# Memory attention of a two-block transformer: queries by features, the query norm in the exponential, two token halves

## The chip, the cores and the metric

The kernel runs on one core of one Trainium2 chip. The metric is the device time of one execution in microseconds (us). The kernel before took 2875.79 us, the median of 3 runs (2870.99 to 2877.94).

## The reference

The input is 512 tokens of 1024 features in fp32. A first block (gated delta rule and dilated window attention) is followed by two layers that each hold a feed-forward network (FFN), a mixer of three attentions, a memory attention, a second FFN and a norm. The change is in the memory attention, which runs once in each of the two layers:

```
h = rms_norm(x, mem_norm_x);  m = rms_norm(mem, mem_norm_m)        # 512 tokens; 256 memory rows
q = rms_norm(per head of (h @ w_q), q_gain)                        # 4 heads of 64
k = rms_norm(per head of k, k_gain);  k, v = split(m @ w_kv)
p = softmax(q k^T * 64**-0.5)                                      # 512 x 256 for each head
x = x + (p v) @ w_o                                                # 256 -> 1024
```

Each rms_norm divides by the square root of the mean square plus 1e-6.

## The kernel before

The residual x lies in the core's memory by features: eight tiles of 128 features by 512 tokens (`X(0)` to `X(7)`). A large product is made of three matmuls for each group of 128 inputs, since weights and activations are each split into a high part, which the matmul takes, and a low rest (`split`, `chunk3`: ScalarE writes the high part, lines 366, 376 and 379, VectorE the rest, lines 367, 377 and 380). `gemm_f` (lines 388 to 390) gives its result by features, `gemm_t` (lines 411 to 413) by tokens. Partial sums have eight banks in three pools: `acc` (3), `ss` (2) and `st` (3).

`Norm` (norm_split) splits x as soon as each `X(k)` is final and adds up its squares on GpSimd (lines 488 and 493); the factor of each token, `norm.cols()`, comes from matmuls with a column of ones (line 434), one small VectorE instruction (424) and a power on GpSimd (425).

`memory` (line 1711), before the change:

- Queries: four products of 128 tokens (three in `acc`, one in `ss`; 96 matmuls of 256 columns). For each of them `query` copies the result out times the token's factor (1726), `head_norm` squares it (1337), reduces by head (1338), takes the power (424, 425) and multiplies (1340), and `place` turns it to features (two transposes, 418) and splits it into `qT` with the gains as scale (379, 380).
- Items: class `Attn` with `per=2` makes eight items, one for each of four token tiles and each of two head pairs (h and h + 2). An item has three stages. Scores: six matmuls of 256 columns, one head after the other, into one `ss` bank (1157 to 1159), one row maximum for both heads (1169), two exponentials with row sums (1172). Turn: four transposes (418) and a VectorE copy (1207). Values: eight records of 64 columns (1224); after both items of a token tile one reciprocal (1234) and one multiplication (1237).
- Output: `turned` transposes and splits each token tile (418, 376, 377); `out(0)` and `out(1)` multiply each half of the tokens with `w_o` (48 matmuls each of 256 columns, 388 to 390, into `acc`) and add into x (1759). `out(0)` is a background generator, stepped between items.

What comes ahead is the mixer's last output product (`out_proj("mla")`, matmuls of 512 columns into `ss`, added into x on line 1658); what comes after is the second FFN, whose first products (lines 400 to 402) need x after `out(1)`. Its weights, and those of w_q and w_o, pass through the same four buffers for high parts, four for low parts and two for raw data.

The order written in the code is not the order on the engines. The framework plans each engine's order ahead with a model of durations: an instruction that is written later goes first where the earlier ones are not ready in that model. On the chip each engine then runs its list in that order.

Of the kernel before, what the change touches and what calls it, by code (L numbers as in the profile page):

```python
# [11 lines left out]
AF = mybir.ActivationFunctionType  # L12
OP = mybir.AluOpType
AX = mybir.AxisListType

T = 512
D = 1024
KD = D // 128
# [4 lines left out]
EPS = 1e-6  # L23
# [7 lines left out]
def _cols(v, n):  # L31
    return np.ascontiguousarray(v.reshape(n, 128).T)
# [96 lines left out]
def prep(I):  # L129
    I = {k: np.asarray(v) for k, v in I.items()}  # L130
    A = {}
# [4 lines left out]
    p = Packer()  # L136
    p.add("ident", np.eye(128))
    p.add("ones", np.ones((128, 128)))
    p.add("norm_w", _cols(I["norm_w"][0], KD))
    for l in range(L2):  # L140
        for n in ("ffn1_norm", "mix_norm", "mem_norm_x", "mem_norm_m", "ffn2_norm", "block_norm", "grp_out_gain"):
# [3 lines left out]
        for n, d in (("mla", 64), ("swa", 64), ("na", 64), ("mem", 64)):  # L145
            for s in "qk":
                g = I[f"{n}_{s}_gain_2"][l]
                if n == "mla":
                    c = np.ones(128, np.float32)
                    c[:64] = g[:64]  # L150
                    p.add(f"{n}{s}r{l}", _rows(g[64:96]))
                else:
                    c = np.concatenate([g, g])
# [5 lines left out]
    t = I["conv_w"][0][:, 0, :]  # L159
    p = Packer()  # L160
# [4 lines left out]
    a = np.arange(128)  # L165
# [7 lines left out]
    p = Packer()  # L173
# [11 lines left out]
    p = Packer()  # L185
    p.add("swab", _bias_swa())
    c, s = _rope_tables(10000.0)
# [5 lines left out]
    w = I["w_in"][0]  # L193
# [5 lines left out]
    o = 2056  # L199
# [42 lines left out]
class Prog:  # L242
# [268 lines left out]
def nat(i):  # L511
    return lambda t: t[:, i * 128:(i + 1) * 128]
# [11 lines left out]
def bc(col, n):  # L524

    return col[:, :, None].to_broadcast([128, col.shape[1], n])
# [6 lines left out]
def hs(h):  # L533
    return slice(h * 128, (h + 1) * 128)
# [796 lines left out]
def head_norm(g, z, nh, d):  # L1331

    nc = g.nc
    sq = g.b()[:, :nh * d]
    zv, sv = z.rearrange("p (h d) -> p h d", h=nh), sq.rearrange("p (h d) -> p h d", h=nh)
    m = g.small(2 * nh)
    nc.scalar.activation(sq, z, AF.Square)
    nc.vector.reduce_sum(m[:, :nh], sv, axis=AX.X)
    g.rsqrt(m[:, nh:2 * nh], m[:, :nh], 1.0 / d)
    nc.vector.tensor_tensor(zv, zv, bc(m[:, nh:2 * nh], d), op=OP.mult)  # L1340


def gain_col(g, name, l, scale):
    t = g.small(1)
    g.nc.vector.scalar_tensor_tensor(t, g.c(f"{name}qg{l}"), scale, g.c(f"{name}kg{l}"), op0=OP.mult, op1=OP.mult)
    return t
# [362 lines left out]


def memory(g, l, xt, mem):
    nc, A = g.nc, g.A
    X = tview(xt)
    norm = g.norm_split(X, g.c(f"mem_norm_x{l}"))
    wh, wl = g.chunk3(A[f"memq{l}"][0], 8)
    qT = g.h(F32R)
    gq = gain_col(g, "mem", l, 0.125)

    def place(i, z):
        ps = g.st()  # L1720
        g.turn(ps, lambda hp: z[:, hs(hp)], 2)
        g.split(ps[:, :256].rearrange("p (k t) -> p k t", k=2), qT[:, :2, hs(i)], qT[:, 2:, hs(i)], gq)

    def query(i, ps):
        z = g.b()[:, :256]
        nc.scalar.activation(z, ps[:, :256], AF.Copy, scale=norm.cols()[:, i:i + 1])
        head_norm(g, z, 4, 64)
        g.later(2, place, i, z)


    pss = [g.acc() for i in range(3)]
    for ks in (range(6), range(6, KD)):
        for i in range(3):
            g.gemm_t(pss[i][:, :256], norm.parts, nat(i), wh, wl, 0, 256, ks)
            if ks[-1] == KD - 1:
                query(i, pss[i])
                g.tick()
    half = lambda t, hb: t[hb * 64:hb * 64 + 64]
    o = g.h()
    hi, lo = g.h(F32R), g.h(F32R)  # L1740
    w = {}

    def turned(i):
        ps = g.st()
        g.turn(ps, lambda c: o[:, i, hs(c)], 2)
        kv = ps[:, :256].rearrange("p (k t) -> p k t", k=2)
        g.split(kv, hi[:, 0:2, hs(i)], lo[:, 0:2, hs(i)])
        if i == 1:
            g.bg.append(out(0))

    def out(hf):
        if not w:
            w["o"] = g.chunk3(A[f"memo{l}"], 2)
        c = slice(hf * 256, hf * 256 + 256)
        parts = [(hi[:, k, c], lo[:, k, c]) for k in range(2)]
        for k in range(KD):
            ps = g.acc()[:, :256]
            g.gemm_f(ps, *w["o"], k * 128, k * 128 + 128, parts)
            nc.vector.tensor_tensor(X(k)[:, c], X(k)[:, c], ps, op=OP.add)
            yield  # L1760

    at = Attn(g, 4, 64, lambda h, i: tuple(half(qT[:, c + h // 2, hs(i)], h % 2) for c in (0, 2)),
              lambda h: [half(t[:, (h // 2) * 256:(h // 2) * 256 + 256], h % 2) for t in mem.kT],
              lambda t, h: mem.v[:, t * 256 + h * 64:t * 256 + h * 64 + 64], lambda i: o[:, i, :256],
              lambda i: (0, 2), None, None, lambda i: g.later(1, turned, i), per=2)
    ps = g.ss()
    g.gemm_t(ps[:, :256], norm.parts, nat(3), wh, wl, 0, 256)
    query(3, ps)
    g.tick()
    g.pipe(at.items(), steps=2)  # L1770
    g.flush()
    for _ in out(1):
        pass
# [98 lines left out]
```

## Time and profile before

| | |
|---|---|
| median of 3 runs | 2875.79 us |
| profiled execution, its own time | 2872.66 us |
| its span, first to last instruction | 2870.9 us |
| mean granted TensorE clock | 0.988 |
| TensorE (PE) busy | 2803.3 us (98%) |
| VectorE (DVE) busy | 1453.1 us (51%) |
| ScalarE (ACT) busy | 1161.7 us (40%) |
| GpSimd (POOL) busy | 459.5 us (16%) |

Some 1.8 us of the profiled execution's time lie outside its span. Busy time of PE is modelled from pipelined matmuls, so that a stretch can read as wholly busy at either level of the clock; a clock of 1.00 is 2.4 GHz, 0.50 is 1.2 GHz. The memory attention lies at 1367 to 1423 us in the first layer and at 2444 to 2493 us in the second.

### The profile page before, as it was taken

To read this page: it belongs to the slowest core of one execution; us is meant where nothing else is said; L and a number is where in the kernel's file an instruction comes from. 1 tells how busy PE (TensorE), PEld (TensorE's weight loads), DVE (VectorE), ACT (ScalarE), POOL (GpSimd) and SP (SyncE) were. 2 spreads that over 40 slices of the span, in tenths; PEclk is the share of its full clock that TensorE was granted. 3 is DMA by queue.
4 is the path that set the end of the run, shared out by engine and by line. 5 is a ranking of instruction groups with operands and counts; after the bars stand their busy time and mean duration, and the time that the engine had idled before them with its cause. 6 is when DMAs were issued, how large, how long until landed. Compare 5 with 4: busy or idle time off the path is not lost.

```text
span 2870.9 us, 37996 instructions
## 1 busy us (share of the span) xinstructions
PE 2803.3 (98%) x15101; PEld 2379.5 (83%) x15101; DVE 1453.1 (51%) x2339; ACT 1161.7 (40%) x2007; POOL 459.5 (16%) x556
## 2 busy tenths in 40 slices
PE   8999999999999999999999999999999999999998
PEld 6798999888888888777888888888888767888887
DVE  5734445445433444677653444533444677653442
ACT  4323444533322234765432224322334766432232
POOL 4422222002000013412200002000013412200001
PEclk9999999999999999999899999999999999999998
DMA  4111222233323232211132323223232211123322
GB/s 162 45 45 60 80 68 74 74 100 126 96 88 103 94 106 68 70 40 64 38 109 86 106 86 105 92 88 107 94 106 67 71 41 65 56 97 88 103 89 80
DMA packets 78466, 239.63 MB, mean 83 GB/s; under 512 B 8528, under 2 KB 14800, under 8 KB 78160
## 3 DMA queue, kind: packets, MB, share of 16 engines
q1 hardware_dynamic: 78288, 237.20, 25.9%
q8 instruction: 119, 1.95, 0.3%
q14 instruction: 59, 0.48, 0.1%
HBM read 235.06 MB, written 2.10 MB: 83 GB/s over the span
## 4 chain that ended last, share of the span: by engine, by line
PE 91%; DVE 4%; ACT 2%; issue 1%; POOL 1%; DMA 0%; SPq 0%; DVEq 0%; ACTq 0%; POOLq 0%
PE ss L388 12%; PE ss L390 12%; PE ss L389 12%; PE acc L388 8%; PE acc L390 8%; PE acc L389 8%; PE acc L411 4%; PE acc L413 4%; PE acc L412 4%; PE st L418 2%; PE acc L1224 2%; PE ss L1260 2%; PE acc L401 1%; PE acc L402 1%; PE acc L400 1%
## 5 line engine op out<-in xcount | busy, mean ns | idle before, releaser
L367 DVE TENSOR_TENSOR wl<-raw,wh 128x1024 fp32r<-128x1024 f32 (+4 forms) x448 | 508.8, 1136 | 563.3 <-ACT wh L366 562.5
L366 ACT ACTIVATE wh<-raw 128x1024 fp32r<-128x1024 f32 (+3 forms) x459 | 450.1, 981 | 725.4 <-PE ss L389 537.2
L388 PE MATMUL acc<-x,wh 128*128 128x512 f32 x1040 | 407.7, 393 | 9.3 <-ACT wh L366 8.8
L390 PE MATMUL acc<-x,wl 128*128 128x512 f32 x1040 | 408.8, 393 | 0.1
L389 PE MATMUL acc<-x,wh 128*128 128x512 f32 x1040 | 407.4, 392 | 0.0
L388 PE MATMUL ss<-h,wh 128*128 128x512 f32 (+1 forms) x843 | 328.9, 391 | 0.3 <-DVE h L1658 0.3
L389 PE MATMUL ss<-h,wh 128*128 128x512 f32 (+1 forms) x843 | 326.3, 389 | 0.2 <-DVE h L380 0.2
L390 PE MATMUL ss<-h,wl 128*128 128x512 f32 (+1 forms) x843 | 325.9, 388 | 0.0
L493 POOL TENSOR_TENSOR b<-b 128x512 f32<-128x512 f32 (+1 forms) x77 | 107.3, 1394 | 1160.7 <-ACT b L488 1069.3
L388 PE MATMUL ss<-x,wh 128*128 128x512 f32 x680 | 264.6, 389 | 0.1
L390 PE MATMUL ss<-x,wl 128*128 128x512 f32 x680 | 264.7, 389 | 0.0
L389 PE MATMUL ss<-x,wh 128*128 128x512 f32 x680 | 264.5, 389 | 0.0
L411 PE MATMUL acc<-wh,x 128*128 128x256 f32 (+1 forms) x880 | 252.8, 288 | 0.0
L412 PE MATMUL acc<-wl,x 128*128 128x256 f32 (+1 forms) x880 | 252.6, 288 | 0.0
L388 PEld LDWEIGHTS acc<-x,wh 128*128 128x128 f32 x1040 | 196.1, 189 | 50.9 <-ACT wh L366 8.8
L413 PE MATMUL acc<-wh,x 128*128 128x256 f32 (+1 forms) x816 | 232.0, 286 | 0.0
L390 PEld LDWEIGHTS acc<-x,wl 128*128 128x128 f32 x1040 | 196.0, 188 | 41.7 <-DVE wl L367 0.9
L389 PEld LDWEIGHTS acc<-x,wh 128*128 128x128 f32 x1040 | 196.0, 189 | 40.3 <-issue 0.3
L388 PEld LDWEIGHTS ss<-h,wh 128*128 128x128 f32 x843 | 159.6, 190 | 33.8 <-DVE h L1658 0.8
L389 PEld LDWEIGHTS ss<-h,wh 128*128 128x128 f32 x843 | 159.8, 190 | 32.7 <-DVE h L380 1.0
L390 PEld LDWEIGHTS ss<-h,wl 128*128 128x128 f32 x843 | 159.7, 189 | 32.0
L1101 ACT ACTIVATE b<-b 128x512 f32<-128x512 f32 x88 | 55.6, 632 | 310.5 <-DVE b L1100 310.4
(384 smaller groups left out, 4756.9 us busy)
## 6 DMA issues: line engine op xcount, KB each, us to landing
raw<-in_ffn_a SPq DMA_DIRECT2D x176, 512.0 KB, 3.6
raw<-in_ffn_b SPq DMA_DIRECT2D x64, 384.0 KB, 3.1
raw<-in_ffn_b SPq DMA_DIRECT2D x64, 320.0 KB, 2.9
raw<-in_w_swa SPq DMA_DIRECT2D x36, 512.0 KB, 3.9
raw<-in_w_gate SPq DMA_DIRECT2D x16, 512.0 KB, 3.6
raw<-in_w_qkv SPq DMA_DIRECT2D x12, 512.0 KB, 4.2
raw<-in_mixN SPq DMA_DIRECT2D x12, 512.0 KB, 3.6
raw<-in_mixA SPq DMA_DIRECT2D x8, 544.0 KB, 3.6
```

Source lines behind the costliest of these rows:

```text
L366: nc.scalar.activation(h[:, s], r[:, s], AF.Copy)
L367: low.tensor_tensor(l[:, s], r[:, s], h[:, s].bitcast(F32), op=OP.subtract)
L388: mm(ps, a, xh, start=first and k == 0, stop=False)
L389: mm(ps, a, xl, start=False, stop=False)
L390: mm(ps, b, xh, start=False, stop=last and k == n - 1)
L411: mm(ps, a, wh[k][:, c0:c1], start=k == 0, stop=False, **part)
L412: mm(ps, a, wl[k][:, c0:c1], start=False, stop=False, **part)
L413: mm(ps, b, wh[k][:, c0:c1], start=False, stop=k == n - 1, **part)
L418: self.nc.tensor.transpose(ps[:, i * 128:(i + 1) * 128], src(i), self.ident)
L493: (engine or nc.gpsimd).tensor_tensor(acc, acc, sq, op=OP.add)
L1224: nc.tensor.matmul(self.pso[:, c:c + d], PT[:, hs(j * n + k)], self.v(lo + k, hj), start=k == 0, stop=k == n - 1)
L1260: nc.tensor.matmul(v3(s), self.q[h // 4][:96, i, hs(h % 4)], self.k[h // 4][:96, :, hs(h % 4)], start=True, stop=True)
```

## The change

Only `memory` changes, and one constant is added: `pair`, 128 rows by 2 columns, which marks the two 64-row heads of a feature tile.

- Queries are made by features with `gemm_f`, in four parts: c (two head pairs: heads 2c and 2c + 1 are the two 64-row halves of the tile) by hf (two halves of 256 tokens). Both c of one hf share one `acc` bank. The result goes unnormalised, times the gains, into `qT`. There is no copy by tokens, no `head_norm` and no transposition of queries.
- The norm's factor: the squares of the raw queries (ScalarE) are summed by head with `pair` as the moving operand (two matmuls of two columns for each part); with e, made from the column sums of the squares of x, one VectorE instruction and one power give f for 2 token tiles by 2 heads. f multiplies the negated row maximum and is the scale of the exponential. `norm.cols()` is not called.
- An item is now a token tile and a feature tile c. Its two heads write two `ss` banks, their matmuls in turn; each has its own row maximum. Reciprocal and multiplication come with every item.
- The order is written out: the items of the first token half stand between pieces of the products of the second half (`nx()`, six matmuls each), those of the second half between pieces of `out(0)`.

```diff
+    def products(c, hf, k0, k1):
+        if (c, k0) == (0, 0):
+            bank[hf] = g.acc()
+        g.gemm_f(bank[hf][:, hh[c]], wh[k0:k1], wl[k0:k1], c * 128, c * 128 + 128, xs[hf][k0:k1], k0 == 0, k1 == KD)
+        if k1 == KD:
+            g.split(bank[hf][:, hh[c]], qT[:, c, hh[hf]], qT[:, 2 + c, hh[hf]], gq)
+            st["sq", c, hf] = sq = g.b()[:, :256]
+            nc.scalar.activation(sq, bank[hf][:, hh[c]], AF.Square)
+
+    def factors(c, hf):
+        if (c, hf) == (0, 0):
+            nc.vector.tensor_scalar(e, g.col_sums(norm.acc, [nat(i) for i in range(4)]), EPS / D, EPS * EPS, op0=OP.mult, op1=OP.add)
+        ps, sq, fc = g.st(), st.pop(("sq", c, hf)), fv(c, hf)
+        for i in range(2):
+            nc.tensor.matmul(ps[:, 2 * i:2 * i + 2], sq[:, hs(i)], pair, start=True, stop=True)
+        two = lambda t: t.rearrange("p (i j) -> p i j", i=2)
+        nc.vector.scalar_tensor_tensor(two(fc), two(ps[:, :4]), 1.0 / 64, bc(e[:, 2 * hf:2 * hf + 2], 2), op0=OP.mult, op1=OP.add)
+        nc.gpsimd.tensor_tensor(fc, fc, g.half.to_broadcast([128, 4]), op=OP.pow)
+
+    def scores(c, i):
+        st["m", c, i] = m = g.small(8)
+        P = st["p", c, i] = g.p()
+        ss = [g.ss()[:, :256] for j in range(2)]
+        for a, b in ((0, 0), (0, 1), (1, 0)):
+            for j, s in enumerate(ss):
+                nc.tensor.matmul(s, half(qT[:, 2 * a + c, hs(i)], j), half(mem.kT[b][:, c * 256:c * 256 + 256], j),
+                                 start=a + b == 0, stop=a == 1)
+        for j, s in enumerate(ss):
+            nc.vector.tensor_reduce(m[:, j:j + 1], s, axis=AX.X, op=OP.max, negate=True)
+        fi = fv(c, i // 2)[:, i % 2 * 2:i % 2 * 2 + 2]
+        nc.vector.tensor_tensor(m[:, 0:2], m[:, 0:2], fi, op=OP.mult)
+        for j, s in enumerate(ss):
+            nc.scalar.activation(P[:, j * 256:j * 256 + 256], s, AF.Exp, bias=m[:, j:j + 1], scale=fi[:, j:j + 1],
+                                 accum_out=m[:, 2 + j:3 + j])
...
+    products(0, 0, 0, KD)
+    products(1, 0, 0, 4)
+    factors(0, 0)
+    scores(0, 0)
+    products(1, 0, 4, KD)
+    w["o"] = g.chunk3(A[f"memo{l}"], 2)
+    unit = iter([(lambda c=c, k=k: products(c, 1, k, k + 2)) for c in range(2) for k in range(0, KD, 2)])
+    nx = lambda: next(unit)()
+    scores(0, 1)
+    nx()
+    turn(0, 0)
+    nx()
+    factors(1, 0)
+    scores(1, 0)
+    turn(0, 1)
+    nx()
+    values(0, 0)
+    scores(1, 1)
+    nx()
...
+    turned(0)
+    scores(0, 3)
+    nx()
+    turned(1)
+    o0 = out(0)
+    turn(0, 2)
+    next(o0)
+    factors(1, 1)
+    scores(1, 2)
+    turn(0, 3)
+    next(o0)
...
+    values(1, 3)
+    turned(2)
+    next(o0)
+    turned(3)
+    next(o0)
     g.flush()
     for _ in out(1):
         pass
```

`turn` (four transposes, VectorE copy) and `values` (matmuls of 64 columns into an `acc` bank) keep their instructions.

## Rows read from the trace of the kernel before

**Rows 1.** The page's busy line.
```profile
PE 2803.3 (98%) x15101; PEld 2379.5 (83%) x15101; DVE 1453.1 (51%) x2339; ACT 1161.7 (40%) x2007; POOL 459.5 (16%) x556
```
**Rows 2.** Busy time by stretch, first layer; then PEclk, DMA share, GB/s.
```profile
1367.29:1376.05 8.76, 8.72 (x73) 8.51 (x71) 3.08 (x5) 3.59 (x5) 2.94 (x3) 1.00 0.18 60
1376.05:1380.79 4.74, 0.00 (x1) 0.04 (x1) 4.30 (x11) 3.69 (x9) 1.62 (x2) 0.97 0.49 156
1380.79:1401.00 20.21, 19.73 (x90) 16.37 (x90) 10.67 (x22) 7.87 (x29) 2.32 (x3) 0.50 0.04 16
1401.00:1422.69 21.69, 21.01 (x171) 20.06 (x171) 14.83 (x30) 8.15 (x20) 2.48 (x2) 1.00 0.01 1
```
**Rows 3.** Busy time by stretch, second layer.
```profile
2443.69:2452.13 8.44, 8.44 (x72) 8.39 (x70) 3.78 (x5) 3.27 (x5) 2.94 (x3) 1.00 0.20 64
2452.13:2457.18 5.05, 0.15 (x2) 0.03 (x1) 3.60 (x11) 4.01 (x9) 1.61 (x2) 0.85 0.54 168
2457.18:2462.60 5.42, 4.94 (x24) 3.38 (x24) 3.36 (x8) 2.38 (x8) 2.33 (x3) 0.51 0.09 37
2462.60:2492.61 30.01, 29.54 (x238) 27.53 (x237) 21.66 (x45) 13.75 (x42) 2.48 (x2) 1.00 0.00 1
```
**Rows 4.** Matmuls in order of time: an early query product; both stages' ends.
```profile
1352.49 0.40 PE L411 MATMUL acc<-wh,x 128*128 128x256 f32 x2
...
1367.29 0.28 PE L411 MATMUL acc<-wh,x 128*128 128x256 f32 x1
...
1422.57 0.28 PE L390 MATMUL acc<-h,wl 128*128 128x256 f32 x1
...
2443.69 0.28 PE L411 MATMUL acc<-wh,x 128*128 128x256 f32 x1
```
**Rows 5.** TensorE's waits: us in total, times, longest.
```profile
PE st L418 <- DVE s L424: 9.7, 2, 4.9
```
**Rows 6.** The chain that ended last, first layer, while TensorE stands.
```profile
1376.05 1.06 ACT wh L366
...
1377.13 1.23 DVE wl L367
1378.36 0.66 DVE s L1338 x2
...
1379.17 2.00 POOL s L425 x2
```
**Rows 7.** Groups of the second layer's stage: count, busy us, mean ns.
```profile
L1207 DVE COPY pt<-st 128x512 f32<-128x512 f32 x8 | 5.4, 681 | 0.7 <-PE st L418 0.6
L1169 DVE TENSOR_REDUCE s<-ss 128x2 f32<-128x512 f32 x8 | 5.3, 684 | 0.9 <-PE ss L1159 0.7
L380 DVE SCALAR_TENSOR_TENSOR h<-st,s,h 128x256 fp32r<-128x256 f32 x4 | 1.9, 480 | 1.4 <-ACT h L379 1.4
L1234 DVE RECIPROCAL s<-s 128x4 f32<-128x4 f32 x4 | 0.7, 166 | 0.0
...
L1172 ACT ACTIVATE p<-ss,s 128x256 f32<-128x256 f32 x16 | 7.5, 474 | 4.3 <-DVE s L1169 4.3
...
L379 ACT ACTIVATE h<-st,s 128x256 fp32r<-128x256 f32 x4 | 1.9, 478 | 2.1 <-PE st L418 2.1
L1337 ACT ACTIVATE b<-b 128x256 f32<-128x256 f32 x4 | 1.7, 414 | 0.1
...
L425 POOL TENSOR_TENSOR s<-s,half 128x4 f32<-128x4 f32 x4 | 3.9, 1010 | 3.5 <-DVE s L424 3.5
```
**Rows 8.** Matmuls in order of time: paired scores (mixer), transposes, values.
```profile
1137.43 0.62 PE L1188 MATMUL ss<-h 64*128 64x256 f32 x6
...
2474.04 1.04 PE L418 MATMUL st<-cst,p 128*128 128x128 f32 x8
...
2475.15 1.89 PE L1224 MATMUL acc<-b,pt 128*128 128x64 f32 x16
```
**Rows 9.** Busy time by stretch in the mixer: a wait, and the clock behind it.
```profile
1190.70:1192.25 1.55, 0.00 (x0) 0.00 (x0) 1.55 (x5) 1.55 (x8) 1.55 (x2) 1.00 0.00 0
1192.25:1196.10 3.85, 3.84 (x16) 3.84 (x17) 3.40 (x15) 3.07 (x12) 2.47 (x3) 0.57 0.73 237
```

More of the change, by code (lines that the diff above doesn't have):

```diff
@@ L138, in prep @@
     p.add("ones", np.ones((128, 128)))
+    p.add("pair", np.arange(128)[:, None] // 64 == np.arange(2))
     p.add("norm_w", _cols(I["norm_w"][0], KD))
@@ L1717, in memory @@
     gq = gain_col(g, "mem", l, 0.125)
[L1719 to L1737, printed above, removed]
+    pair = g.c("pair")
+    f = g.small(16)
+    fv = lambda c, hf: f[:, 8 * hf + 4 * c:8 * hf + 4 * c + 4]
+    e = g.small(4)
+    st = {}
+    hh = [slice(0, 256), slice(256, 512)]
+    xs = [[(a[:, c], b[:, c]) for a, b in norm.parts] for c in hh]
+    bank = {}
+    def products(c, hf, k0, k1):
[15 more added lines that the diff above has]
+        nc.gpsimd.tensor_tensor(fc, fc, g.half.to_broadcast([128, 4]), op=OP.pow)
     half = lambda t, hb: t[hb * 64:hb * 64 + 64]
@@ L1741, in memory, with turn, values @@
     w = {}
+    def scores(c, i):
[13 more added lines that the diff above has]
+                                 accum_out=m[:, 2 + j:3 + j])
+    def turn(c, i):
+        P, t = st.pop(("p", c, i)), g.st()
+        g.turn(t, lambda k: P[:, hs(k)])
+        st["t", c, i] = PT = g.pt()
+        nc.vector.tensor_copy(PT, t)
+    def values(c, i):
+        PT, m = st.pop(("t", c, i)), st.pop(("m", c, i))
+        ps = g.acc()[:, :128]
+        for j in range(2):
+            v = (2 * c + j) * 64
+            for k in range(2):
+                nc.tensor.matmul(ps[:, j * 64:j * 64 + 64], PT[:, hs(2 * j + k)], mem.v[:, k * 256 + v:k * 256 + v + 64],
+                                 start=k == 0, stop=k == 1)
+        nc.vector.reciprocal(m[:, 4:6], m[:, 2:4])
+        dst = o[:, i, hs(c)]
+        hv = lambda t: t.rearrange("p (j d) -> p j d", j=2)
+        nc.vector.tensor_tensor(hv(dst), hv(ps), bc(m[:, 4:6], 64), op=OP.mult)
     def turned(i):
@@ L1747, in turned @@
         g.split(kv, hi[:, 0:2, hs(i)], lo[:, 0:2, hs(i)])
-        if i == 1:
-            g.bg.append(out(0))
     def out(hf):
-        if not w:
-            w["o"] = g.chunk3(A[f"memo{l}"], 2)
-        c = slice(hf * 256, hf * 256 + 256)
+        c = hh[hf]
         parts = [(hi[:, k, c], lo[:, k, c]) for k in range(2)]
@@ L1760, in out @@
             yield
[L1762 to L1770, printed above, removed]
+    products(0, 0, 0, KD)
[17 more added lines that the diff above has]
+    nx()
+    turn(1, 0)
+    values(0, 1)
+    nx()
+    factors(0, 1)
+    turn(1, 1)
+    values(1, 0)
+    nx()
+    scores(0, 2)
+    values(1, 1)
+    nx()
+    turned(0)
+    scores(0, 3)
+    nx()
+    turned(1)
[6 more added lines that the diff above has]
+    next(o0)
+    values(0, 2)
+    scores(1, 3)
+    next(o0)
+    turn(1, 2)
+    values(0, 3)
+    next(o0)
+    turn(1, 3)
+    next(o0)
+    values(1, 2)
+    next(o0)
+    values(1, 3)
+    turned(2)
+    next(o0)
+    turned(3)
+    next(o0)
     g.flush()
```

## The prediction

> **What bounds the kernel now.** The page comes first: TensorE is busy for 98% of the span [rows 1], so what moves the time is TensorE standing still, running at the lower clock, or doing less. The table of stretches then shows the memory attention, which I take from the first query product behind the mixer's last output matmul to the last matmul of the output product [rows 4]: 8.76 + 4.74 + 20.21 + 21.69 = 55.40 us in the first layer, 8.44 + 5.05 + 5.42 + 30.01 = 48.92 us in the second [rows 2, 3], together 104.3 us or 3.6% of the span. In both layers TensorE runs dry for about 5 us, then runs at 0.50 (1.2 GHz) for 20.21 or 5.42 us before it is back at 1.00 (2.4 GHz). The list of waits names the gap: twice, 4.9 us at the longest, the transposition of the queries waits for the small VectorE instruction of the head norm [rows 5]. The chain shows what lies in it: a splitting of FFN weights (1.06 + 1.23 us), two reductions, two powers of 1 us [rows 6].
>
> The lower clock has a price that these two layers give, since the code is the same: from the gap's end on, the first takes 41.90 us and the second 35.43, 6.47 us more for 14.79 us more at half clock, 0.44 us for each. Without gap and half clock the stage would take 55.40 - 4.74 - 0.44 x 20.21 = 41.8 us and 48.92 - 5.05 - 0.44 x 5.42 = 41.5 us. The two agree, and 41.7 us is my base.
>
> **The change, part by part.** All is for one layer.
>
> *The gap goes.* From the last query product to the first score there were nine steps with two powers one behind the other. Now the scores need only the split of 256 tokens (0.48 us on ScalarE, 0.48 on VectorE [rows 7]). Squares, two-column matmuls and one power (1.01 us [rows 7]) run beside the scores' matmuls, and the second half's 48 product matmuls of 0.12 us (8.76 us for 73 records [rows 2]), 5.8 us, are there to run meanwhile. That exceeds the 2.5 us from square to factor: 0.41 + about 0.4 + 0.17 + 1.01 and handovers. So the base stands without the gap. If that cover is gone, the factor's chain costs up to 2.5 us.
>
> *TensorE's work.* Eight transposes of queries go: 8 x 0.11 = 0.9 us (seven steps in 1.04 - 0.28 us for eight records [rows 8]; 0.28 us is one matmul's own length [rows 4]). The query products stay 96 matmuls of 256 columns, weights and tokens having only changed sides. The scores of two heads now sit on different halves of the rows and alternate, as in the mixer, where six take 0.62 us, 0.07 apart [rows 8], against 0.12 apart one after the other: 0.4 instead of 0.72 us, eight times, -2.5 us. The sums by head and pair add 16 records; by the values' step, (1.89 - 0.28) / 15 = 0.107 us [rows 8], +1.7 us. Sum -1.7 us.
>
> *The shared bank, new.* Both c of one token half lie in one bank. In these rows no product writes a bank that another engine still reads, so the trace doesn't show whether c = 1 can run while c = 0 is read. If it can, 0 us. If not, each of two banks has to be read first: split and square, 0.48 + 0.48 + 0.41 = 1.4 us, 2.8 us together. I take 2.8, since at the stage's start little else is ready: the planner spends ready products early, as the query product at 1352.49 us in the middle of the mixer's output shows [rows 4]. The Trainium skill has a rule against this layout (PSUM — Partial Sum Buffer, "PSUM bank collisions raise a hardware error"): a matmul may not write a bank while ScalarE or VectorE reads it, even in other columns, so a semaphore has to guard the whole bank. By it the cost is the 2.8 us that I took, without it 0; no row here shows it.
>
> *One item in flight, new.* An item now fills both `ss` banks, so the next item's scores wait for this one's exponentials: 0.62 (scores) + 0.7 (two maxima; one over twice the width took 0.684) + 0.17 + 2 x 0.47 (exponentials) + about 0.2 for handovers = 2.65 us [rows 7, 8]. Eight make 21.2 us. Begun some 5 us into the stage, followed by the last item's tail (4.3 us, below) and the last output product (48 x 0.12 = 5.8 us), that ends at 36 us, inside the base. So it costs nothing while VectorE answers at once. If every item also waits for one copy (0.68 us) and one weight subtraction (1.23 us), 1.9 us more, the chain ends at 36.3 + 15.3 = 51.6 us. I take the near end, since VectorE is busy 21.66 of 30 us in that stretch [rows 3], and keep the other as a rival.
>
> *The tail, new.* Before, `out(0)` was still there to run while the last item finished. Now its pieces stand between the items. Behind the last exponential come four transposes (0.7 us), copy (0.68), values (1.0), reciprocal (0.17), product (at most 0.48), two transposes (0.4), split (0.96): 4.3 us. The item ahead's values and perhaps two pieces of `out(0)` cover about 2 us. I take +2.3, between 0 and 4.3.
>
> *Nothing else.* The weights of `w_o` are asked for earlier in the text, but the planner had them early before. Reciprocals and products per item rather than per tile add some 2 us to VectorE, beside TensorE's work. The powers fall from five to four.
>
> Sum: 41.7 - 1.7 + 2.8 + 2.3 = 45.1 us a layer, 90.2 for two against 104.3: 14.1 us less. The profiled execution's own 2872.66 us becomes 2858.6; the median of the runs lies 3.1 us above that execution, so on it 2861.7, say 2862 us.
>
> **The rivals.**
>
> *The clock falls all the same.* In the mixer a wait of 1.55 us is followed by most of 3.85 us at half clock (0.57) [rows 9], so it takes no 5 us gap. The bank's reads or the tail could do it. At 10 us of half clock a layer, between the two layers of before, it costs 2 x 10 x 0.44 = 8.8 us and leaves a gain of 5.3: 2870 us. Against it: the work around is dense.
>
> *The pace of the items becomes the bound.* Then a layer takes 51.6 us, both 103.2, and the gain is 1 us: 2875. For it: one item in flight, and the planner may place FFN weights ahead of the split, as it did in the gap [rows 6], so that the written order doesn't come out. Against it: VectorE has some 28% free.
>
> *Slower: short waits at every item hold the clock down.* Place: from the first exponential to the last `turned`, both layers, 27 us each. Each item leaves TensorE up to 1 us dry (2.65 us a round against 0.4 + 0.44 + 0.84 of its own work), and at half clock the same stretch is TensorE's bound, so nothing is won back. Price 54 x 0.44 = 23.7 us: 9.6 us slower, 2885 us. It decides above 14.1 / 0.44 = 32 us of half clock over both layers. For it: the first layer stayed down for 20.21 us although TensorE showed 19.73 us of work [rows 2]. Against it: the second came back after 5.42 us with the same code [rows 3].
>
> **How the numbers follow.** Forecast 0.50, falling clock 0.20, pace 0.15, slower 0.15. 0.3% is 8.6 us, about what a measurement of this kernel can tell from no change. Faster by more: 0.95 of the forecast, 0.4 of the falling clock, a quarter of the pace: 0.60. Slower by more: nearly all of the last: 0.14. Same: 0.26. The low end takes both unknown costs at 0 and half of the pace's slack, 10 us below the forecast: 2852. The high end takes in the falling clock and the pace with some loss: 2880. Outside lie most of the slower case and a little below.
>
> **What would show it.** Right: the stretches of 5 us without matmuls are gone, the granted clock stays 1.00 from 1367 to about 1412 us, the stage is 44 to 46 us in both layers, the score matmuls overlap in pairs, and the row for waits on line 424 is gone. The bank is settled by whether products of c = 1 begin before the square of c = 0 has ended. The pace shows as maxima 2.7 us apart, or 4.5 for the rival. Wrong: a clock of 0.50 for over 16 us a layer, or a stage above 50 us. Time that moves by more than 3 us outside both stages would upset the sum too.

## The result, and the profile after

The kernel after takes 2897.75 us (median; 2892.31 to 2902.35; one disturbed run of 11872.19 us is left aside) against 2875.75 us for the kernel before beside it: ratio 1.0074, 95% interval 1.0061 to 1.0086. It is slower by 22 us, where 14 us faster was forecast. The profiled execution has a span of 2894.0 us against 2870.9.

The page's busy line of after, which answers to [rows 1]: TensorE is busy for 22 us more, although the change takes work from it.

```profile
PE 2825.2 (98%) x15117; PEld 2394.7 (83%) x15117; DVE 1453.9 (50%) x2371; ACT 1161.0 (40%) x1999; POOL 455.5 (16%) x554
```

The stretches of the stage, first layer and then second, answer to [rows 2, 3]. Columns: stretch, its length, busy us and count of PE, PEld, DVE, ACT, POOL, granted clock, DMA share, GB/s.

```profile
1368.43:1380.00 11.57, 9.56 (x70) 8.16 (x69) 5.58 (x14) 5.07 (x12) 2.92 (x3) 1.00 0.13 46
1380.00:1392.00 12.00, 10.20 (x74) 8.74 (x74) 7.70 (x20) 6.13 (x15) 2.02 (x2) 1.00 0.29 88
1392.00:1412.50 20.50, 20.03 (x82) 16.59 (x82) 8.47 (x26) 5.08 (x18) 1.01 (x1) 0.51 0.01 1
1412.50:1429.71 17.21, 15.98 (x122) 14.81 (x123) 11.11 (x25) 7.04 (x15) 2.49 (x2) 0.99 0.00 1
2454.61:2460.50 5.89, 4.57 (x34) 3.81 (x33) 3.61 (x6) 3.38 (x6) 1.91 (x2) 1.00 0.25 89
2460.50:2464.50 4.00, 4.00 (x22) 4.00 (x22) 0.82 (x3) 0.00 (x0) 0.78 (x1) 0.57 0.02 4
2464.50:2477.50 13.00, 10.38 (x76) 8.89 (x75) 7.39 (x19) 7.26 (x19) 1.24 (x2) 1.00 0.23 71
2477.50:2498.50 21.00, 19.74 (x81) 16.34 (x80) 8.50 (x25) 4.31 (x14) 2.01 (x2) 0.51 0.02 7
2498.50:2518.86 20.36, 18.36 (x137) 16.50 (x138) 12.87 (x31) 8.24 (x19) 2.49 (x2) 1.00 0.00 1
```

The stage takes 61.28 and 64.25 us, where it took 55.40 and 48.92: 21.2 of the 23.1 us by which the span grew. No stretch of 5 us without matmuls is left, and yet the clock reads 0.51 for about 20 us in each layer, and in the second for some 3.4 us more early on. No wait of several us precedes the fall. The longest of TensorE's waits (columns: us in total, times, longest) is 1.0 us in the first layer, whose four longest come first here, and 1.5 us in the second, the last row; the row on line 424 of [rows 5] is gone:

```profile
PE ss L1762 <- ACT p L1769: 1.7, 2, 1.0
PE acc L1784 <- DVE pt L1776: 1.5, 2, 0.8
PE acc L389 <- ACT h L377: 0.9, 2, 0.5
PE acc L390 <- DVE x L381: 0.8, 1, 0.8
...
PE acc L1784 <- DVE pt L1776: 3.8, 4, 1.5
```

Two numbers per stage serve below. *Half clock* is the time at 1.2 GHz, counted in stretches of 0.5 us by the granted clock of each. *At full clock* is the length less 0.44 us for each us of half clock. That price holds: in the eleven kernels below whose two layers differ by 6.8 us or more of half clock, the difference in length is 0.39 to 0.54 of it (e1: 4.53 / 10.2 = 0.44). By this range a length at full clock is uncertain by up to 0.1 us for each us of half clock, 2 us where that is 20 us; between two stages only the difference of their half clock counts. So before is 46.4 and 45.9 us at full clock with 20.5 and 6.8 us of half clock, after 52.3 and 53.7 us with 20.5 and 23.9 us. Of the 21.2 us, 0.44 x (44.4 - 27.3) = 7.5 us are clock and 13.7 us are a longer stage at full clock.

Part of what makes it longer shows in TensorE's order (columns: start, us, matmul, output and inputs, count, wait ahead of it). The six score matmuls of the first item alternate between the heads; from the second item on they are torn into three and three, with other matmuls between, since each head's bank comes free by itself:

```profile
1372.57 1.05 PE L435 MATMUL st<-cst,b 128*128 128x1 f32 x8 [0.40 <-POOL b L494]
1373.55 0.62 PE L1762 MATMUL ss<-b,h 64*128 64x256 f32 x6
1374.10 0.39 PE L389 MATMUL acc<-x,wh 128*128 128x256 f32 x1
...
1375.64 0.50 PE L1745 MATMUL st<-cst,b 128*128 128x2 f32 x4
1376.00 0.36 PE L389 MATMUL acc<-x,wh 128*128 128x256 f32 x1
...
1378.37 0.62 PE L1762 MATMUL ss<-b,h 64*128 64x256 f32 x3 [0.70 <-ACT p L1769]
1378.92 0.44 PE L419 MATMUL st<-cst,p 128*128 128x128 f32 x2
1379.29 0.62 PE L1762 MATMUL ss<-b,h 64*128 64x256 f32 x3
...
1383.71 0.62 PE L1762 MATMUL ss<-b,h 64*128 64x256 f32 x3
```

From start to next start, six alternating matmuls take 1374.10 - 1373.55 = 0.55 us, three of one head take 1378.92 - 1378.37 = 0.55 us as well. All seven later items of both layers are torn, so an item costs 1.10 us at full clock. In the kernel before, where the six of an item stand in one piece, one head after the other, they take 2463.63 - 2462.73 = 0.90 us:

```profile
2462.73 0.38 PE L1157 MATMUL ss<-b,h 64*128 64x256 f32 x1
...
2463.63 0.69 PE L418 MATMUL st<-cst,p 128*128 128x128 f32 x4
```

The first items of the first layer follow each other by 4.8 to 5.3 us (1373.55, 1378.37, 1383.71); over both stages, half clock included, it is 4.4 to 9.1 us, where 2.65 was forecast.

### The profile page after: what moved, and what is told of

Its sections match the earlier page's. It is cut to its first block, busy times and chain, and to the rows that moved or that the text cites. A ratio compares the mean times of both kernels' runs of the same rounds, so it can differ in the third digit from the quotient of the medians.

```text
span 2894.0 us, 38037 instructions
## 1 busy us (share of the span) xinstructions
PE 2825.2 (98%) x15117; PEld 2394.7 (83%) x15117; DVE 1453.9 (50%) x2371; ACT 1161.0 (40%) x1999; POOL 455.5 (16%) x554
## 4 chain that ended last, share of the span: by engine, by line
PE 92%; DVE 3%; ACT 2%; POOL 1%; issue 1%; DMA 0%; SPq 0%; DVEq 0%; ACTq 0%; POOLq 0%
PE ss L389 12%; PE ss L390 12%; PE ss L391 12%; PE acc L389 9%; PE acc L390 9%; PE acc L391 9%; PE acc L412 4%; PE acc L414 4%; PE acc L413 4%; PE st L419 3%; PE ss L1261 1%; PE acc L1225 1%; PE acc L402 1%; PE acc L403 1%; PE acc L401 1%; PE acc L1289 1%
## 5 line engine op out<-in xcount | busy, mean ns | idle before, releaser
L389 PE MATMUL acc<-x,wh 128*128 128x512 f32 (+1 forms) x1104 | 426.5, 388 | 10.3 <-ACT wh L367 9.6
L390 PE MATMUL acc<-x,wh 128*128 128x512 f32 (+1 forms) x1104 | 426.1, 386 | 1.6 <-DVE x L381 1.6
L391 PE MATMUL acc<-x,wl 128*128 128x512 f32 (+1 forms) x1104 | 426.7, 387 | 0.1
L389 PEld LDWEIGHTS acc<-x,wh 128*128 128x128 f32 x1104 | 208.7, 189 | 53.4 <-ACT wh L367 9.6
L390 PEld LDWEIGHTS acc<-x,wh 128*128 128x128 f32 x1104 | 209.0, 189 | 42.4 <-DVE x L381 2.0
L391 PEld LDWEIGHTS acc<-x,wl 128*128 128x128 f32 x1104 | 208.7, 189 | 41.6 <-DVE wl L368 0.9
L412 PE MATMUL acc<-wh,x 128*128 128x256 f32 (+1 forms) x832 | 239.9, 288 | 0.0
L413 PE MATMUL acc<-wl,x 128*128 128x256 f32 (+1 forms) x832 | 239.8, 288 | 0.0
L414 PE MATMUL acc<-wh,x 128*128 128x256 f32 (+1 forms) x768 | 219.7, 286 | 0.0
```

What stands on the lines that cost most here:

```text
L389: mm(ps, a, xh, start=first and k == 0, stop=False)
L390: mm(ps, a, xl, start=False, stop=False)
L391: mm(ps, b, xh, start=False, stop=last and k == n - 1)
L412: mm(ps, a, wh[k][:, c0:c1], start=k == 0, stop=False, **part)
L413: mm(ps, a, wl[k][:, c0:c1], start=False, stop=False, **part)
L414: mm(ps, b, wh[k][:, c0:c1], start=False, stop=k == n - 1, **part)
```

## The experiments

All times below are medians; "stage" gives both layers' lengths, and half clock and length at full clock behind it. Kernels of one batch (e1 to e4, e5 to e8, e9 to e12, e13 to e15, e16 and e17) ran on one chip beside the kernel before, whose median moved from 2875.40 to 2878.67 us between batches. Kernels of different batches are therefore compared by their ratios, times 2876 us.

| kernel | ratio to before, interval | stage | half clock | at full clock |
|---|---|---|---|---|
| before | 1 | 55.40, 48.92 | 20.5, 6.8 | 46.4, 45.9 |
| after | 1.0074 [1.0061, 1.0086] | 61.28, 64.25 | 20.5, 23.9 | 52.3, 53.7 |
| e1 row pairs | 1.0005 [0.9992, 1.0017] | 47.83, 52.36 | 0, 10.2 | 47.8, 47.9 |
| e2 after, plain order | 1.0109 [1.0088, 1.0130] | 69.06, 69.96 | 30.7, 34.1 | 55.5, 55.0 |
| e3 row pairs, plain order | 1.0046 [1.0027, 1.0064] | 55.94, 58.61 | 17.1, 23.9 | 48.4, 48.1 |
| e4 before, gap filled | 1.0053 [1.0035, 1.0072] | 61.35, 57.21 | 27.3, 17.1 | 49.3, 49.7 |
| e5 row pairs, own banks | 1.0033 [1.0021, 1.0045] | 58.48, 54.81 | 27.3, 20.5 | 46.5, 45.8 |
| e6 after, one bank of two pools | 1.0042 [1.0027, 1.0057] | 60.80, 57.87 | 27.3, 20.5 | 48.8, 48.9 |
| e7 after, own banks | 1.0102 [1.0082, 1.0122] | 68.35, 63.66 | 37.6, 27.3 | 51.8, 51.7 |
| e8 after, no factor | 1.0076 [1.0056, 1.0095] | 62.67, 66.78 | 27.3, 37.5 | 50.7, 50.3 |
| e9 after, 8 unread an item | 1.0044 [1.0028, 1.0060] | 58.64, 58.67 | 3.4, 3.4 | 57.1, 57.2 |
| e10 row pairs, 8 unread | 1.0024 [1.0014, 1.0033] | 55.67, 55.72 | 3.4, 3.4 | 54.2, 54.2 |
| e11 row pairs, own banks, 4 unread | 0.9982 [0.9973, 0.9991] | 48.62, 48.63 | 0, 0 | 48.6, 48.6 |
| e12 before, 8 unread | 1.0067 [1.0051, 1.0084] | 64.63, 60.50 | 23.9, 13.6 | 54.1, 54.5 |
| e13 row pairs, own banks, 2 unread | 0.9971 [0.9952, 0.9990] | 50.66, 50.78 | 10.2, 10.2 | 46.2, 46.3 |
| e14 before, gap filled and 8 unread | 1.0083 [1.0059, 1.0107] | 61.39, 67.01 | 6.8, 20.5 | 58.4, 58.0 |
| e15 after, own banks, 4 unread | 1.0097 [1.0074, 1.0120] | 66.92, 65.13 | 30.7, 30.7 | 53.4, 51.6 |
| e16 after, own banks, 8 unread | 1.0060 [1.0040, 1.0079] | 62.83, 59.29 | 17.1, 10.2 | 55.3, 54.8 |
| e17 row pairs, own banks, 3 unread | 0.9984 [0.9968, 0.9999] | 47.69, 47.56 | 0, 0 | 47.7, 47.6 |

The stage of each table row comes from one profiled execution, the ratio from all runs. Two of these executions lie far from their kernel's median: e6's took 2897.15 us (median 2890.41), e16's 2888.23 us (median 2895.86).

### The items' banks and the written order (e1 to e4)

e1 makes an item of the two heads of one row half, so that it needs one `ss` bank and one maximum. Both query products of a token half stand ahead of its first item; the rest of the written order stays:

```diff
-        ss = [g.ss()[:, :256] for j in range(2)]
...
+        s2 = g.ss()
+        for c in range(2):
+            for a, b in ((0, 0), (0, 1), (1, 0)):
+                nc.tensor.matmul(s2[:, c * 256:c * 256 + 256], half(qT[:, 2 * a + c, hs(i)], r), ...)
+        nc.vector.tensor_reduce(m[:, 0:2], s2.rearrange("p (j k) -> p j k", j=2), axis=AX.X, op=OP.max, negate=True)
```

> The changed kernel with one part undone: an item is again a pair of heads on the same row half (h and h + 2), whose scores go into one ss bank, so that two items can be in flight. The written order stays, except that both head tiles of a token half are made before its first item. Theory A (pace: two ss banks for each item leave one item in flight, and the queue behind it stands): most of the 22 us over the kernel before goes, 2865 to 2880 us, and the row maxima come closer than the 4.7 to 9 us apart of the changed kernel. Theory B (order: the planner's mix of product pieces, transposes and values ahead of scores that are ready holds the items up): 2888 to 2900 us. Theory C (clock: about 45 us at 1.2 GHz against 26 before, 0.44 us lost for each, is all that counts): time follows the half-clock stretch, which this edit need not shorten; 2890 us or more.

e2 and e3 take the written order out of after and of e1 (all products first, then the items through the pipeline helper of before):

```diff
-    unit = iter([(lambda c=c, k=k: products(c, 1, k, k + 2)) for c in range(2) for k in range(0, KD, 2)])
...
+    g.pipe([(st3(scores, c, i), st3(turn, c, i), st3(last, c, i)) for i in range(4) for c in range(2)], steps=2)
```

> The changed kernel with its written order undone: all products, all factors, then the eight items through the plain pipeline that the kernel before used (turn two items behind the scores, values three), with the first half of the output as background steps. Items still fill two ss banks. Theory A (one item in flight): stays at 2885 to 2900 us. Theory B (the written order): back to 2865 to 2880 us. Theory C (clock): follows the half-clock stretch.

> Both undone: one ss bank for each item and the plain pipeline. What is left of the change is the arithmetic: queries by features, no head norm by tokens, the factor in the exponential. By the prediction's own sum this is the base without the gap, 41.7 us a layer, with 2.8 us for the shared bank and less work by 1.7 minus nothing for paired scores: about 44 us a layer, 2860 to 2868 us, if neither A nor B nor the clock stands in the way. Theory C: if the clock still falls in the items, 2870 to 2885 us.

e4 is the kernel before with 40 matmuls ahead of the items whose results nobody reads, in its gap:

```diff
+    fill = g.acc()[:, :256]
+    for n in range(40):
+        nc.tensor.matmul(fill, norm.parts[n % KD][0][:, :128], wh[n % KD][:, :256], start=n == 0, stop=n == 39)
```

> The kernel before with 40 matmuls of 256 columns added in each layer behind the last query product, whose sums nobody reads: 4.8 us of work where TensorE ran dry for 4.7 and 5.05 us. Theory C (half clock costs 0.44 us a microsecond): no half clock in the two stages, 25.6 x 0.44 = 11 us less, 2863 to 2867 us. If the price is not the clock's but that of the chain of waits, 2873 to 2879 us, as before.

e1 takes some 20 us off after, and is level with before. The two layers of e1:

```profile
1368.64:1416.47 47.83, 45.04 (x344) 40.70 (x343) 31.12 (x75) 23.08 (x58) 8.39 (x8) 1.00 0.10 34
2445.38:2497.74 52.36, 49.57 (x344) 44.88 (x342) 31.15 (x75) 23.05 (x58) 8.40 (x8) 0.90 0.09 31
```

With as many matmuls as after (344), TensorE stands 2.8 us instead of 5.5 and 7.2. In its list of waits the values are gone, and scores wait 0.2 us, once. At full clock the stage is 4.5 and 5.8 us shorter. The serial scores of an item stay in one piece, 0.97 us:

```profile
1383.99 0.97 PE L1762 MATMUL ss<-b,h 64*128 64x256 f32 x6
```

The written order isn't the loss: without it after is 10 us slower and e1 12 us, by 0.2 to 3.2 us a layer at full clock and by 20 and 31 us of half clock over both layers. In e2 and e3 TensorE stands 2.5 and 2.4 us at the factor's matmuls, for the square, and the clock falls there.

e4 was meant to show whether the gap loses the clock in the kernel before. Its first layer, with the waits on line 424 gone:

```profile
1367.05:1384.50 17.45, 14.94 (x124) 14.30 (x122) 9.24 (x20) 8.50 (x16) 6.88 (x7) 1.00 0.12 40
1384.50:1412.50 28.00, 27.99 (x126) 24.48 (x127) 13.27 (x26) 8.97 (x35) 0.00 (x0) 0.51 0.09 32
1412.50:1428.40 15.90, 15.43 (x127) 14.96 (x126) 10.80 (x22) 5.85 (x11) 2.49 (x2) 1.00 0.01 2
```

The fill stands in the long gap, and the clock reads 1.00 through it. Behind it TensorE still waits twice, ahead of the first scores, for the split of the queries:

```profile
PE ss L1157 <- ACT h L379: 1.3, 1, 1.3
PE ss L1159 <- DVE h L380: 1.0, 1, 1.0
```

The clock falls just behind these two waits, for about 27 us, and the kernel is 15 us slower. So the base of the prediction, the stage "without gap and half clock", isn't what one gets by closing the long gap. Since a rest of that gap is left ahead of the fall, e4 alone doesn't show that the items lose the clock; e14, below, leaves waits of 0.5 us at most there.

### Bank, pool and factor, each by itself (e5 to e8)

e5 and e7 give each query product a bank of its own, in e1 and in after; e6 takes the second head's bank from the other pool, so that two items can be in flight; e8 leaves the query norm out, its matmuls as well as its chain:

```diff
-            bank[hf] = g.acc()
+            bank[c, hf] = g.acc()[:, :256]
```

```diff
-        ss = [g.ss()[:, :256] for j in range(2)]
+        ss = [t()[:, :256] for t in (g.ss, g.st)]
```

> The row-pair kernel (2880 us, stages of 47.8 and 52.4 us) with one more part undone: each of the four query products has an acc bank of its own. If the shared bank costs what the prediction took (2.8 us a layer), the products of the second head tile begin before the squares of the first have been read, and the stage at full clock falls from 47.8 to about 45 us, 2873 to 2877 us in all. If it is hidden, the stage stays at 47 to 48.5 us and the time at 2878 to 2883.

> The changed kernel, order and pairs of heads as they are, but the second head's scores go into an st bank, so that two items can be in flight. Theory A (one item in flight): of the 5 to 6 us a layer that the changed kernel loses against the row-pair kernel at full clock, most comes back, stages of 47 to 50 us without the half clock; 2880 to 2888 us. If not the banks but the pairing of heads or the written order is the cause: 2894 to 2900 us, as changed. st has three banks, so the transposes may wait instead: 2888 to 2895.

> The changed kernel with a bank of its own for each of the four query products, nothing else. With the cost that the prediction took: 2.8 us less a layer, 2889 to 2893 us. If the items' pace sets the end: within 2 us of the changed kernel, 2894 to 2899.

> The changed kernel without the norm's factor: the squares, their sums by head, the column sums and the powers are left out, and f is a constant, so the attention weights differ. If the factor's chain is hidden, as predicted, only TensorE's share goes, 1.7 to 2.5 us a layer, 2892 to 2896 us. If the first exponentials wait for it (in the changed kernel's trace the first maximum stands 2.1 us behind a small VectorE instruction of the factor, and the first exponential waits for the power): 4 to 6 us a layer, 2884 to 2890 us.

Each makes the stage shorter at full clock, and none makes the kernel faster by as much. Own banks save 1.3 and 2.1 us a layer on e1, 0.5 and 2.0 on after. Two items in flight save 3.5 and 4.8 us on after. The factor, left out, saves 1.6 and 3.4 us. Since half clock differs by 3 to 27 us within these pairs, the price leaves 0.3 to 2.7 us of each saving open. But own banks cost some 8 us over the whole run, in e5 against e1 and in e7 against after, since half clock grows by 20 to 38 us over both layers. The order changed too: here 40 of the products stand ahead of the first scores and none right behind them, and TensorE stands for the first exponentials, once in each layer of e5 (first row) and of e7 (second row):

```profile
PE st L419 <- ACT p L1768: 3.1, 1, 3.1
PE ss L1762 <- ACT p L1769: 2.2, 1, 2.2
```

The first fall comes within that wait in e5 and within 2 us behind it in e7. The first layer of e6 shows the clock best, with three falls in one stage:

```profile
1371.10:1377.50 6.40, 5.09 (x36) 4.33 (x35) 3.61 (x6) 3.38 (x6) 1.90 (x2) 1.00 0.22 83
1377.50:1384.50 7.00, 7.00 (x33) 6.54 (x32) 1.41 (x5) 1.63 (x5) 1.01 (x1) 0.51 0.00 0
1384.50:1387.50 3.00, 2.62 (x19) 1.98 (x17) 1.83 (x6) 1.79 (x7) 0.00 (x0) 1.00 0.02 5
1387.50:1395.00 7.50, 7.50 (x35) 6.73 (x34) 2.56 (x8) 2.26 (x5) 1.01 (x1) 0.54 0.00 0
1395.00:1405.00 10.00, 9.71 (x69) 8.11 (x69) 8.09 (x22) 5.80 (x17) 1.01 (x1) 1.00 0.33 105
1405.00:1419.00 14.00, 14.00 (x63) 13.21 (x64) 5.31 (x17) 2.53 (x9) 1.01 (x1) 0.51 0.01 2
1419.00:1431.90 12.90, 12.43 (x102) 11.96 (x101) 9.72 (x20) 5.84 (x11) 2.48 (x2) 1.00 0.00 1
```

And these are all of TensorE's waits in the same stage of e6, 2.4 us together:

```profile
PE acc L390 <- DVE x L381: 0.8, 1, 0.8
PE ss L1762 <- ACT p L1769: 0.7, 2, 0.4
PE acc L389 <- ACT h L377: 0.5, 1, 0.5
PE st L435 <- POOL b L494: 0.4, 1, 0.4
```

The clock falls three times, and the longest wait is 0.8 us. The Trainium skill ("TensorE: Matmul & The Clock Gate", section "A second HAM failure mode: psum-queue depth-cycling") tells of a kernel that goes through PSUM banks and stops TensorE shortly between groups of matmuls, so that its clock goes to and fro; these rows agree as to the clock and the short waits, but that the waits are the cause isn't shown.

### Unread matmuls among the items (e9 to e17)

The last question was whether the items themselves lose the clock. These kernels put matmuls of 256 columns, read by nobody, ahead of each item's values in the written order, 0.12 us each at full clock and so about 1 us a layer for each one in an item (n is the number in the table):

```diff
-        ps = g.acc()[:, :128]
+        t = g.acc()
+        ps = t[:, :128]
+        for n in range(8):
+            nc.tensor.matmul(t[:, 256:], mem.kT[0][:, :128], mem.kT[0][:, :256], start=True, stop=True)
```

> The kernel after, with eight matmuls of 256 columns ahead of each item's values whose results nobody reads (about 8 x 0.12 = 0.96 us an item, 7.7 us a layer at full clock). So far every kernel lost the clock among the items, where TensorE does short matmuls with short waits, also where the gap ahead of them was filled. Theory (the sparse items lose the clock): with the items filled, half clock falls from 20.5 and 23.9 us a layer to under 7, the stage is 53 + 7.7 less what fills waits (up to 5), 56 to 61 us a layer, and the kernel takes no longer than the one after, 2885 to 2897 us. Rival (the clock's falls do not hang on the items' density): half clock stays at 20 us and more, and the kernel is some 10 to 15 us slower than after, about 2910 us.

> The row-pair kernel (both heads of an item in one bank, one pair after the other) with the same eight matmuls of unread result ahead of each item's values, 7.7 us a layer. It had 0 and 10.2 us of half clock in the two stages and 47.8 us a layer at full clock in one profile, but its runs spread over 10 us. Theory: half clock near 0 in both stages, the stage 54 to 55.5 us in both, the kernel about 2885 us with a smaller spread. Rival: half clock of 10 us and more in either stage, the kernel about 2890 us.

> The row-pair kernel with a bank for each query product, and four matmuls of unread result ahead of each item's values (3.8 us a layer). Without them it had the shortest stage at full clock, 46.5 and 45.8 us, and 27.3 and 20.5 us of half clock, 2885.7 us. Theory: half clock goes to under 7 us a stage, the stage is 50 us, and the kernel gains (47.8 - 14) x 0.44 - 7.7 = 7 us on that: 2878 us, level with the kernel before. Rival: half clock stays, 2885.7 + 7.7 = 2893 us.

> The kernel before, with eight matmuls of unread result ahead of each item's values in the memory attention (7.7 us a layer). It has 20.5 and 6.8 us of half clock, behind a gap of 5 us. Theory (items decide): half clock under 7 us in both stages, the stage 46 + 7.7 = 54 us in both, 2876 + (55.4 + 48.9 against 108), so 2880 us. Rival (the gap alone loses the clock in this kernel, and the items only keep it down): half clock of 6 to 20 us as before, the kernel at 2876 + 15 = 2891 us.

e9 does 7.7 us a layer more than after and is some 9 us faster (2887.77 us): half clock went from 44.4 to 6.8 us, and its runs have a mean clock of 0.988 to 0.992, after's 0.981 to 0.987. TensorE also stands less, 3.5 us a stage instead of 5.5 and 7.2. The stages of e9, and then of e11, which takes 2872.82 us:

```profile
1367.76:1426.40 58.64, 55.12 (x406) 49.86 (x404) 32.64 (x83) 23.27 (x58) 8.42 (x8) 0.97 0.08 28
2448.99:2507.66 58.67, 55.15 (x406) 49.96 (x404) 32.65 (x83) 23.27 (x58) 8.42 (x8) 0.97 0.08 28
```

```profile
1370.06:1418.68 48.62, 47.36 (x373) 43.90 (x372) 30.98 (x75) 22.93 (x58) 8.41 (x8) 1.00 0.10 34
2441.93:2490.56 48.63, 47.37 (x374) 43.91 (x372) 30.99 (x75) 22.94 (x58) 8.42 (x8) 1.00 0.09 33
```

With the same half clock in both, the two layers of a kernel agree within 0.05 us (e9, e10, e11), where those of before lay 6.5 us apart. e11 has 3.8 us a layer of useless work, and beats both kernels: e5, the same without it, was 2885.68 us. This pair doesn't test the items alone, since the planned order changed with the filling: where e5 stands 3.1 us for the first exponentials, e11 has eight unread matmuls and 24 products, and its longest wait is 0.5 us, as in e13 and e17. e10 kept 6.8 us of half clock where e1 had 10.2; its 15.4 us of useless work over both layers cost the run some 5 us. e12 missed: in the kernel before, the same filling left 23.9 and 13.6 us of half clock. Sixteen of its unread matmuls stand in the gap, of which a wait of 1.7 us is left, and the clock falls there.

> The row-pair kernel with a bank for each query product and two matmuls of unread result ahead of each item's values instead of four (1.9 us a layer instead of 3.8). With four, both stages took 48.6 us with no half clock, and the kernel 0.9982 of before. Theory: what counts is how TensorE is occupied among the items, and two are nearly enough: half clock 0 to 4 us a stage, the stage 47 to 48.5 us, the kernel 2869 to 2872 us. Rival: the clock falls as without fill (27 and 20 us a stage), 2883 to 2886 us.

> The kernel before with both fills at once: 40 unread matmuls ahead of the items (they stood in its gap of 5 us) and 8 ahead of each item's values. The first alone left 27.3 and 17.1 us of half clock, the second alone 23.9 and 13.6 us. Theory (gap and sparse items each lose the clock on their own): half clock under 4 us a stage, the stage 49.5 + 7.7 less what the fill covers, 55 to 57 us in both layers. Rival (something else in this kernel's items loses the clock): half clock of 13 us and more, the stage above 62 us.

> The kernel after with a bank for each query product, and four unread matmuls ahead of each item's values. Beside the row-pair kernel with the same fill and banks (48.6 us a stage, no half clock) it differs only in that an item's heads fill two ss banks. Theory: half clock under 7 us a stage, and the stage longer by the price of one item in flight, 3 to 6 us: 52 to 55 us, the kernel 2880 to 2886 us. Rival (the two banks cost nothing of themselves, only through the clock): the stage 48.6 us too, and the kernel 2873 us.

e14 and e15 missed, and by its stages e13 (10.2 us of half clock a stage, 50.7 us) lies between its two theories. Before with both fills still lost the clock, for 6.8 us in the first layer and 20.5 in the second, behind waits of 0.5 us at most. After with own banks and four unread matmuls lost it in both (0.77 and 0.76); there the first unread matmuls themselves wait 1.6 us for a bank that the square still reads. The second layer of e14:

```profile
2452.19:2473.00 20.81, 19.78 (x156) 18.30 (x155) 12.04 (x25) 10.84 (x25) 6.88 (x7) 1.00 0.22 75
2473.00:2494.00 21.00, 21.00 (x93) 18.42 (x91) 7.12 (x15) 4.64 (x19) 0.00 (x0) 0.51 0.01 2
2494.00:2519.20 25.20, 23.69 (x192) 22.73 (x192) 14.02 (x29) 8.05 (x20) 2.49 (x2) 1.00 0.00 1
```

e13's twelve runs fall into two groups: four at 2857.43 to 2858.54 us with a mean clock of 0.995, eight at 2871.42 to 2875.05 us with 0.986 to 0.988. Its profile is one of the slower group; where the other's clock stayed up wasn't seen. In the first layer of this profile the clock falls although TensorE had no wait in the 7 us ahead:

```profile
1385.50:1392.50 7.00, 7.00 (x58) 6.34 (x57) 5.18 (x15) 2.13 (x8) 1.99 (x2) 1.00 0.25 75
1392.50:1403.00 10.50, 10.07 (x43) 8.51 (x43) 4.34 (x15) 4.63 (x16) 0.00 (x0) 0.51 0.01 2
```

> The kernel after with a bank for each query product and eight unread matmuls ahead of each item's values (7.7 us a layer; four left 30.7 us of half clock in both stages). Theory (their number decided): half clock under 7 us a stage, the stage 55 to 58 us, the kernel 2882 to 2888 us, 15 to 20 us less than with four. Rival (own banks themselves lose the clock here): half clock stays above 20 us, the stage 68 us and more, the kernel above 2900 us.

> The row-pair kernel with a bank for each query product and three unread matmuls an item. With two, a run had either a mean clock of 0.995 and 2857 to 2859 us or 0.986 to 0.988 and 2871 to 2875 us; with four, 0.989 to 0.992 and 2868 to 2876 us. Theory (each unread matmul makes a fall in the items rarer and costs 0.96 us a layer): no half clock in the stages, 47.5 us each, the runs mostly at 2860 to 2872 us, median about 2868 us. Rival (which level a run takes hangs on something else in the program): the runs are split in two as with two, with the median at 2873 us.

e16 lies between its two theories: eight instead of four took half clock from 61.4 to 27.3 us (in the fastest of its four runs) and the run some 11 us down, not 15 to 20. e17 has no half clock in either stage and 47.6 us, as its theory had it, with runs between 2865.01 and 2879.52 us without a cut in two; at 2870.78 us it isn't told apart from e11 and e13. These three are the versions that beat the kernel before, by 0.2 to 0.3%, and after by 26 to 30 us.

## Why the prediction was wrong

**"The gap goes. So the base stands without the gap."** The first half came true: the waits on line 424 are gone. The second is the step that failed. The base was taken as what the stage takes without gap and half clock, and the forecast kept the clock at 1.00. Half clock went from 27.3 to 44.4 us over both layers instead of to 0. At 0.44 this is 0.44 x 44.4 / 2 = 9.8 us a layer beyond the forecast. The prediction read [rows 2, 3] as one cause, the gap, and one effect. e4 closes the long gap and has more half clock, and e14, with its items filled too, still falls behind waits of 0.5 us at most: the gap was not all that loses the clock. e9 shows by an experiment that in after the place is its own items: with them filled, half clock went from 44.4 to 6.8 us. By which of its effects the filling works, its matmuls or the 2.0 and 3.7 us less of standing, it doesn't show.

**"TensorE's work", -1.7 us.** The eight transposes of queries are gone. The paired scores came out for one item in eight. The text alternates the heads, but each head has its own bank, and the order on the engine takes up each head as its bank comes free. The term set 8 x 0.4 = 3.2 us against 8 x 0.72 = 5.8 before. By the starts above it is 0.55 + 7 x 1.10 = 8.3 us, and before took 8 x 0.90 = 7.2: 1.1 us more where 2.5 less were forecast, an error of 3.6 us a layer. The prediction took the step of a long run of equal products, 0.12 us; in a group of six scores it is 0.90 / 6 = 0.15 us. The torn matmuls are shown by the rows; since no experiment keeps two banks and an untorn item, this size is worked out, not measured.

**"One item in flight costs nothing."** It costs standing time: 5.5 and 7.2 us against 2.8 in e1, which has one bank for each item. With a second item in flight (e6) the stage at full clock is 3.5 and 4.8 us shorter, and e1, which also keeps its items whole, is 4.5 and 5.8 us shorter. The prediction added up the chain score, maximum, exponential, and left out that the next scores also stand in TensorE's order behind six product matmuls, transposes and values. Together with the torn scores this makes the stage 53.0 us at full clock where 45.1 was forecast.

**"The shared bank", 2.8 us.** Right in kind, too large: products of c = 1 began at 1374.10 us, after the square of c = 0 had ended (1373.06 + 0.38 = 1373.44), in these rows of ScalarE:

```profile
1371.97 0.84 ACT L380 ACTIVATE h<-acc,s 128x256 fp32r<-128x256 f32 x2 [1.38 <-PE acc L391]
1373.06 0.38 ACT L1738 ACTIVATE b<-acc 128x256 f32<-128x256 f32 x1 [0.25 <-DVE h L381]
1377.67 0.56 ACT L1769 ACTIVATE p<-ss,s 128x256 f32<-128x256 f32 x1 [4.23 <-DVE s L1767]
```

By e5 and e7 a bank of its own is worth 0.5 to 2.1 us a layer; e9 and e16, which differ in the same way, are 1.8 and 2.4 us apart at full clock. The order in the trace agrees with the Trainium skill's rule that was cited ahead (PSUM — Partial Sum Buffer, "PSUM bank collisions raise a hardware error"). Own banks were the slower choice all the same, by the clock.

**The factor's chain beside the scores.** It was costed at nothing behind the products. ScalarE stands 4.23 us until the maximum times the factor is there, as the last row shows: the scores were done at about 1374.2, but the matmuls that add up the squares stood behind 12 products (1375.64 us), and VectorE's maximum behind them. TensorE, with products to run, stands only 0.70 us for it (1378.37). e8 is 1.6 and 3.4 us shorter at full clock, but it also lacks the matmuls of the factor: 1373.55 - 1372.57 = 0.98 us for the column sums and four times about 0.4 us (1376.00 - 1375.64 = 0.36), 2.6 us together. So nothing beyond TensorE's own work is shown by it. Where the cover is gone the chain does cost, as the prediction said, with up to 2.5 us: in e5 and e7 TensorE stands 3.1 and 2.2 us.

**"The tail", +2.3 us.** Not measured by itself. The rows show 0.9 us of standing for the split on line 377 in after's first layer.

**Outside the stages** 1.9 us were lost. Ahead of the first stage 1.1 us were lost. Between the stages the time grew from 1021.0 to 1024.9 us, with 17 us of half clock in the second layer's mixer instead of 3.4, and behind them it fell by 3.1 us.

**The rivals.** What came is the slower one with the pace on top. "Short waits at every item hold the clock down" was to decide above 32 us of half clock; 44.4 came, and the price of 0.44 held; that short waits are what holds the clock down isn't shown. The pace was put at 51.6 us a layer and 4.5 us from maximum to maximum; 53.0 us at full clock came, and items 4.4 to 9.1 us apart. The prediction looked for the cause in VectorE; e6, where the banks let two items be in flight, is 3.5 and 4.8 us shorter with the same work on VectorE. Each had a chance of 0.15, and they were counted as alternatives, though both come from the same place, the items.

**Left open.** Why a stage falls to 1.2 GHz in one execution and not in another (e13), and why the filling that worked in e9 to e11 and e17 did not in e12, e14 and e15. Waits of 1.3 to 3.1 us stand in or close ahead of a fall in e2 to e5, e7, e12 and e15, of 1.5 us in after's second layer. But e13 fell without one, and standing time over a stage doesn't order the kernels: e6 stood 2.5 us and had 27.3 us of half clock, e9 3.5 us and had 3.4. Nor is it settled how much of e11, e13 and e17 is the filling and how much the other order that came with it.

## What to carry to other kernels

Where a stage has run at half clock, do not subtract that time together with the gap ahead of it: ask whether the work that is left keeps the clock up, and price both cases. Before an item is given two banks, count how many items can then be in flight, and look in the engine's order for whether what was written as alternating stays so. A saving at full clock of a few us is only worth what the clock leaves of it: here taking some 2 us off each stage at full clock made the kernel some 8 us slower (e5, e7), and 4 us a stage of useless matmuls, with the other order that came with them, made it some 15 us faster (e11 against e5).

## What was not expected of the hardware

The clock went to 1.2 GHz with no wait over 0.8 us in a stage that TensorE spent 58.35 of 60.80 us busy by its records (e6), and once down it stayed there for about 7, 7 and 14 us, in e4 for 27. In e13 it fell after 7 us in which TensorE was busy throughout by its records. The spread of a kernel's runs goes with the mean clock: after's go from 2892.31 us at a mean clock of 0.987 to 2902.35 us at 0.981, e13's from 2857.43 us at 0.995 to 2875.05 us at 0.986. With the same half clock in both, the stage repeats within 0.13 us from layer to layer (e9, e10, e11, e17).
